# Column sums of the modulation on VectorE beside the feed-forward, and the two scan directions of the linear attention in pairs

## The chip, the cores and the metric

The kernel runs on one core of one Trainium2 chip. The metric is the time on the device of one execution, in microseconds (us), less is better.

## What is computed

Two layers of a diffusion backbone work on 256 latent tokens (x) and 256 context tokens (ctx) of width 1024. Each layer needs six modulation rows of 1024 numbers (shift, scale and gate ahead of the mixer, and the same three ahead of the feed-forward), made from a conditioning vector. Layer 0 needs them for two conditionings (c for x, c_ctx for ctx). Layer 1 drops the context after the mixer, so its last three rows are needed for c alone.

```python
def modulation(cond, w, b):
    return jnp.split(jax.nn.silu(cond) @ w + b, 6, axis=-1)
...
    for i in range(DEPTH):
        last = i == DEPTH - 1
        sh1, sc1, gt1, sh2, sc2, gt2 = [m[:, None, :] for m in modulation(c, w_ada[i], b_ada[i])]
        csh1, csc1, cgt1, csh2, csc2, cgt2 = modulation(c_ctx, w_ada[i], b_ada[i])
        h = rmsnorm(x, g_pre_mix[i]) * (1.0 + sc1) + sh1
        hc = rmsnorm(ctx, g_pre_mix[i]) * (1.0 + csc1) + csh1
        y, yc = mixer(h, hc, w_in[i], w_out[i], gla_w_gate[i], gla_b_gate[i], gla_g_norm[i], na_rpb[i], not last)
        x = x + gt1 * rmsnorm(y, g_post_mix[i])
        h = rmsnorm(x, g_pre_ffn[i]) * (1.0 + sc2) + sh2
        x = x + gt2 * rmsnorm(channel_mixer(i, h), g_post_ffn[i])
```

The mixer projects the tokens and runs two groups of heads on them: gated linear attention in chunks of 64 tokens, forward and backward in the sequence, each direction with a running state S that is scaled by a decay and added to once per chunk; and neighbourhood attention (a softmax over a window of the grid and all context keys). The channel mixer is a dense SwiGLU in layer 0 and eight SwiGLU experts, two chosen per token, in layer 1. All weights are float32.

## The kernel before

All of it is one program of five engines, each of which takes its instructions strictly in order: TensorE (PE), VectorE (DVE), ScalarE (ACT), GpSimd (POOL) and SyncE (SP), which issues nearly all transfers. A scheduler sets the order of each engine from the order in which the code is written, except in stretches that are marked as written out by hand. Two generators are interleaved by `weave(main, filler, each)`: after each `yield` of the main one, `each` steps of the filler are taken.

**Weights.** A weight arrives as a float32 piece `raw` of 128 x 1024 numbers (0.5 MB) in a ring of five buffers. For most products it is split into a rounded part `wr` (ACT, line 169) and the rest `wl` (DVE, line 170), three buffers of each, and a product of 512 columns is three matmuls (`mm3`, lines 210 to 212) with the activations' parts `HR` and `HL`.

**Modulation.** `ada_rows` (line 344) makes 512 columns of the 6144, named by j from 0 to 11: it loads four raw pieces of `w_ada` and multiplies them, unsplit, with the conditionings in `condS` on PE: eight matmuls of 32 output rows each (line 354), in float32, which the profile records twice each. `ada_cols` copies the rows (line 359), turns them into columns with four transpositions (line 371), and adds up four partial rows and the bias on DVE (lines 373, 374). `ada_gate` makes the gate (j = 4, 5 or 10, 11): the row is spread over all partitions by matmuls with `selbc` (line 418), the bias and the gain are put in on DVE and POOL (lines 420, 421). Before the change layer 1's columns are made in three places: j = 0 to 3 beside the dense feed-forward of layer 0; j = 4, 5 in layer 1's projections and linear attention; j = 6 to 9 and then 10, 11 beside layer 1's neighbourhood attention.

**Stages in order of time**, with the us of the profiled span: start (0 to 60), layer 0's projections and linear attention (60 to 200), neighbourhood attention (200 to 300), output projection (300 to 350), dense feed-forward, its first part (350 to 615) and its second (615 to 745); layer 1's projections (745 to 815), linear attention (815 to 895), neighbourhood attention (895 to 957), output projection with the router (957 to 996), experts (996 to 1898).

**Start.** `start` is written by hand: x arrives in four tiles; each is normalised (line 1881 on ACT and what follows it) and turned on PE (line 1889). The first modulation columns come in four quarters (lines 1852, 1860), each turned into scale and shift, and then the first projection begins (line 210). `clear_rel` fills a tile `far` with -1e30 and writes it over two tables in DRAM, 1.5 MB each, by GpSimd's own transfers (line 331).

**Linear attention** (`core`, in `gla_parts`). Its items are pairs of a direction d and a token tile of 128 tokens, two chunks in each. Step s1 makes decays E, s2 the products inside a chunk, s3 (line 787) adds to the output bank: values (line 797), then per chunk two matmuls with the state (line 804) and four DVE operations that advance it (line 816).

**Neighbourhood attention** (`natt`). Of an item (two heads b, one of them j, 128 queries), `n1` makes the scores (lines 899, 900), adds the window's bias (904), takes the maximum (907) and the exponential on ACT (910); `n1b` divides by the sum (916, 917); `n2` transposes (927) and copies (928); `n3` multiplies with the values (942), and `na_done` writes the result (1002, 1003). Every second pair of heads needs operands that `prep` makes (875 to 879). Layer 1 has 16 items. Its filler is `sr` (the projection r), then LAG steps of `fill`, `o_turns` (line 1056, the linear attention's output transposed), and the rest of `fill`; `RATE` says how many filler steps come after each step (their values stand in the diff below).

**Dense feed-forward**, first part: 40 pieces of weights with 24 matmuls each, two yields a piece, one filler step after each yield. **Experts**: weights stream through a ring of up to 27 buffers; the first are asked for when the output projection's last piece is at hand.

## Time and profile before

| | |
|---|---|
| median of 3 runs | 1898.14 us (1897.8 to 1899.89) |
| the profiled execution, its own time | 1900.5 us |
| its span, first to last instruction | 1898.6 us |
| PE busy | 1821.3 us, 96% of the span |
| DVE busy | 1124.8 us, 59% |
| ACT busy | 926.7 us, 49% |
| mean granted clock of TensorE | 0.989 of full speed |
| bytes moved | 492 MB, of which 352 MB are expert weights |

A matmul's recorded time contains its way through the array, so recorded times of neighbours overlap and a busy PE is a sum without the overlap. The share of an engine is an average over stages with different limits; what a stage is bound by is read from the stage.

### The profile page before, as it was taken

The numbers are of one execution on the slowest core, as the hardware profiler recorded it, in microseconds if no ns is written. First come the engines' busy times: TensorE is split into PE (matmuls) and PEld (weight loads), VectorE is DVE, ScalarE is ACT, GpSimd is POOL, SyncE is SP. The second block draws the span as 40 slices with busy tenths as digits, with TensorE's granted clock in tenths as the row PEclk, the third lists the DMA queues.
The fourth block names the chain that finished last, engine by engine and source line by source line (L and its number), as shares of the span: only waits on it lengthen the run. The fifth ranks groups of instructions, "written<-read, shape, count | busy, mean of one in ns | idle before, by whom it ended". The sixth has DMA issues, their size and how long they took to land. (4 is left out here: it accounts for less than half of the span.)

```text
span 1898.6 us, 25634 instructions
## 1 busy us (share of the span) xinstructions
PE 1821.3 (96%) x8929; PEld 1300.5 (68%) x8929; DVE 1124.8 (59%) x1636; ACT 926.7 (49%) x1336; POOL 84.6 (4%) x101
## 2 busy tenths in 40 slices
PE   5999999999999999999989999999999999999995
PEld 2687666867887887787467863488887348888731
DVE  4456876422223335367768961399997239999701
ACT  3442366522222336433647851377775237777501
POOL 2100200010000002001010000000000000000000
PEclk9999999999999999999989999999999999999998
DMA  9432645266332331434789989999999999999996
GB/s 324 136 103 52 195 166 200 78 200 199 89 100 89 114 116 53 146 90 123 243 309 358 340 319 411 413 413 409 414 381 344 411 408 413 410 413 381 342 410 254
DMA packets 203305, 492.16 MB, mean 259 GB/s; under 512 B 29665, under 2 KB 71169, under 8 KB 203169
## 3 DMA queue, kind: packets, MB, share of 16 engines
q1 hardware_dynamic: 201152, 483.12, 69.7%
q0 software_dynamic: 2016, 7.34, 1.2%
q8 instruction: 72, 1.18, 0.3%
q14 instruction: 65, 0.52, 0.1%
HBM read 486.20 MB, written 4.98 MB: 259 GB/s over the span
## 5 line engine op out<-in xcount | busy, mean ns | idle before, releaser
L170 DVE TENSOR_TENSOR wl<-raw,wr 128x1024 fp32r<-128x1024 f32 x446 | 536.6, 1227 | 227.3 <-ACT wr L169 221.6
L169 ACT ACTIVATE wr<-raw 128x1024 fp32r<-128x1024 f32 x446 | 466.3, 1059 | 301.9 <-PE ps L211 145.1
L210 PE MATMUL ps<-wr,HR 128*128 128x512 f32 x736 | 298.1, 405 | 2.7 <-ACT wr L169 2.6
L211 PE MATMUL ps<-wl,HR 128*128 128x512 f32 x736 | 291.0, 395 | 4.5 <-DVE wl L170 3.4
L212 PE MATMUL ps<-wr,HL 128*128 128x512 f32 x736 | 290.6, 395 | 0.0
L210 PE MATMUL ps<-HR,wr 128*128 128x512 f32 (+1 forms) x592 | 222.6, 377 | 9.4 <-ACT HR L1903 6.0
L211 PE MATMUL ps<-HL,wr 128*128 128x512 f32 (+1 forms) x592 | 219.6, 371 | 2.9 <-DVE HL L1908 1.5
L212 PE MATMUL ps<-HR,wl 128*128 128x512 f32 (+1 forms) x592 | 218.3, 369 | 0.0
L211 PEld LDWEIGHTS ps<-wl,HR 128*128 128x128 f32 x736 | 139.1, 189 | 41.8 <-DVE wl L170 11.4
L210 PEld LDWEIGHTS ps<-wr,HR 128*128 128x128 f32 x736 | 139.2, 189 | 37.7 <-ACT wr L169 4.9
L212 PEld LDWEIGHTS ps<-wr,HL 128*128 128x128 f32 x736 | 139.0, 189 | 32.0 <-issue 0.8
L210 PEld LDWEIGHTS ps<-HR,wr 128*128 128x128 f32 x592 | 112.1, 190 | 46.6 <-issue 15.8
L211 PEld LDWEIGHTS ps<-HL,wr 128*128 128x128 f32 x592 | 112.2, 189 | 24.1 <-DVE HL L1908 3.4
L212 PEld LDWEIGHTS ps<-HR,wl 128*128 128x128 f32 x592 | 112.2, 190 | 19.8
L1524 PE MATMUL ps<-raw,xw 128*64 128x512 f32 (+1 forms) x596 | 117.2, 537 | 1.6 <-DMA raw<-in_moe_w_gate 0.8
L210 PE MATMUL ps<-wr,tr 128*128 128x512 f32 x280 | 111.9, 400 | 0.0
L211 PE MATMUL ps<-wl,tr 128*128 128x512 f32 x280 | 110.8, 396 | 0.0
L212 PE MATMUL ps<-wr,tl 128*128 128x512 f32 x280 | 110.6, 395 | 0.0
L1539 DVE TENSOR_TENSOR hid<-hid,ps 128x512 f32<-128x512 f32 (+1 forms) x47 | 31.3, 665 | 133.0 <-PE ps L1524 133.0
L1524 PEld LDWEIGHTS ps<-raw,xw 128*64 128x64 f32 x596 | 40.7, 137 | 65.9 <-issue 53.6
L1524 PE MATMUL ps<-raw,tw 128*64 128x512 f32 x272 | 66.4, 604 | 5.7 <-DMA raw<-in_moe_w_down 4.2
L212 PEld LDWEIGHTS ps<-wr,tl 128*128 128x128 f32 x280 | 52.6, 188 | 12.8
(353 smaller groups left out, 2423.8 us busy)
## 6 DMA issues: line engine op xcount, KB each, us to landing
raw<-in_moe_w_down SPq DMA_DIRECT2D x180, 512.0 KB
raw<-in_moe_w_gate SPq DMA_DIRECT2D x169, 512.0 KB
raw<-in_moe_w_up SPq DMA_DIRECT2D x167, 512.0 KB
raw<-in_w_ada SPq DMA_DIRECT2D x80, 512.0 KB
raw<-in_w_in SPq DMA_DIRECT2D x48, 512.0 KB
HR1w<-in_moe_w_up SPq DMA_DIRECT2D x24, 512.0 KB
raw<-in_ffn_w_gate SPq DMA_DIRECT2D x22, 512.0 KB
raw<-in_ffn_w_up SPq DMA_DIRECT2D x22, 512.0 KB
```

Source lines behind the costliest of these rows:

```text
L169: nc.scalar.activation(wr, raw, AF.Copy)
L170: nc.vector.tensor_tensor(out=wl, in0=raw, in1=wr.bitcast(F32), op=ALU.subtract)
L210: nc.tensor.matmul(o, lr, rr, start=start, stop=False)
L211: nc.tensor.matmul(o, lr, rl, start=False, stop=False)
L212: nc.tensor.matmul(o, ll, rr, start=False, stop=stop)
L1524: nc.tensor.matmul(o[a * HALF:(a + 1) * HALF, 0:n], x, raw[:, a * n:(a + 1) * n], start=start, stop=stop)
L1539: nc.vector.tensor_tensor(out=hid, in0=hid, in1=st.pop((fb, 1))[:, 0:w], op=ALU.mult)
```

## The change

Four things change. **First**, layer 1's modulation columns j = 0 to 3 and 6 to 11 (not 4 and 5) leave PE: `ada_wide` takes the raw pieces beside the dense feed-forward of layer 0, and DVE multiplies each piece's 512 columns by the conditioning's number of that partition and adds it to a sum tile (lines 403, 405; one operation for each k of 8 and each conditioning: 112 in all). Four sums at a time are then added over the 128 partitions by matmuls with a tile of ones (line 409). Shifts and scales are turned as before, but for four sums at once (`wide_cols`); the gate goes through two rows in DRAM, from where it is spread over the partitions in layer 1 (`wide_gate`, `load_gate`). The 24 pieces of `w_ada` for j = 6 to 11 thereby move from layer 1's neighbourhood attention into the feed-forward; the number of pieces stays the same. **Second**, `s3` takes both directions of a step together: eight value matmuls, then for each half step the state matmuls of one direction and the other in turn. The decays are copied out of E (12 small copies on DVE), and the core has 20 yields where it had 24. **Third**, layer 1's neighbourhood attention has `RATE` (.65, 40, .65) and LAG 0, and its filler no longer has modulation in it. **Fourth**, `clear_rel` is called in the pool of the start and not ahead of it.

```diff
+    def ada_wide(pool, groups):
+        for l, js, conds, done in groups:
+            combos = [(j, c) for j in js for c in conds]
+            tiles = [pool.tile([P, D], F32, tag="t4", name="sums") for _ in range((len(combos) + 1) // 2)]
+            acc = {jc: tiles[i // 2][:, i % 2 * 512:(i % 2 + 1) * 512] for i, jc in enumerate(combos)}
+            for j in js:
+                for u in range(4):
+                    raw = wraw(kview(A["w_ada"][l], u, slice(j * 512, (j + 1) * 512)), 2)
+                    yield
+                    for kk in (2 * u, 2 * u + 1):
+                        for c in conds:
+                            i_, s_, o = raw[:, kk % 2 * 512:(kk % 2 + 1) * 512], condS[:, kk, c:c + 1], acc[j, c]
+                            if kk == 0:
+                                nc.vector.tensor_scalar(out=o, in0=i_, scalar1=s_, scalar2=None, op0=ALU.mult)
+                            else:
+                                nc.vector.scalar_tensor_tensor(out=o, in0=i_, scalar=s_, in1=o, op0=ALU.mult, op1=ALU.add)
+            yield
+            bank = ps()
+            for i, jc in enumerate(combos):
+                nc.tensor.matmul(bank[32 * i:32 * i + 32, :], ones, acc[jc], start=True, stop=True)
+            yield from done(l, js, conds, bank)
+    def wide_cols(l, js, conds, bank):
+        rows = ad.pool.tile([P, 512], F32, tag="adarows", bufs=2, name="adarows")
+        nc.scalar.activation(rows, bank, AF.Copy)
+        yield
+        pc = ps()
+        for c4 in range(4):
+            nc.tensor.transpose(pc[:, c4 * P:(c4 + 1) * P], rows[:, c4 * P:(c4 + 1) * P], ident)
+        n = len(js)
+        o = modc[l][:, 4 * js[0]:4 * js[0] + 4 * n, :].rearrange("p (j a) b -> p j a b", j=n)
+        i_ = pc.rearrange("p (a j x) -> p j a x", a=4, j=n)[:, :, :, 0:33:32] if len(conds) == 2 else \
+            pc.rearrange("p (a j x) -> p j a x", a=4, j=n)[:, :, :, 0:1].to_broadcast([P, n, 4, 2])
+        b_ = bcol[:, l, 4 * js[0]:4 * js[0] + 4 * n].rearrange("p (j a) -> p j a", j=n)
+        for q in range(n):
+            nc.vector.tensor_tensor(out=o[:, q], in0=i_[:, q], in1=b_[:, q].unsqueeze(2).to_broadcast([P, 4, 2]), op=ALU.add)
+        yield
+    gate_rows = dp.tile([2, 512], F32, name="gate_rows")
+    def wide_gate(l, js, conds, bank):
+        bb, gb = (ad.pool.tile([P, 512], F32, tag=t, bufs=n, name=t) for t, n in (("bb", 2), ("gb", 1)))
+        for i, j in enumerate(js):
+            r = slice(32 * i, 32 * i + 32)
+            nc.gpsimd.dma_start(bb[r], A["b_ada"][l:l + 1, j * 512:(j + 1) * 512].to_broadcast([32, 512]))
+            nc.gpsimd.dma_start(gb[r], A["g_post"][2 + l:3 + l, i * 512:(i + 1) * 512].to_broadcast([32, 512]))
+        yield
+        rows = ad.pool.tile([P, 512], F32, tag="adarows", bufs=2, name="adarows")
+        for t, i_ in ((bb, bank), (gb, rows)):
+            nc.vector.tensor_tensor(out=rows[0:64], in0=i_[0:64], in1=t[0:64], op=ALU.add if t is bb else ALU.mult)
+        for i in range(2):
+            nc.gpsimd.dma_start(gate_rows[i:i + 1, :], rows[32 * i:32 * i + 1, :])
+        yield
+    def load_gate(gt):
+        gt[0] = gtb()
+        nc.gpsimd.dma_start(gt[0], gate_rows.rearrange("a b -> (a b)").unsqueeze(0).to_broadcast([P, D]))
         yield
...
+                Es = gc.tile([P, 2, 2], F32, tag="Es", bufs=3, name="Es")
+                at = P + (63 if d == 0 else 0)
+                nc.vector.tensor_copy(Es, E[:, :, at:at + 65:64])
+                it["dec"] = lambda hpi, c: Es[:, hpi, c:c + 1]
...
-            def s3(it):
-                d, tt, step = it["d"], it["tt"], it["step"]
+            def values(it):
+                d, tt = it["d"], it["tt"]
...
+            def s3(pair):
+                for it in pair:
+                    values(it)
+                for i in range(2):
+                    cs = [(it, i if it["d"] == 0 else 1 - i) for it in pair]
                     for hpi in range(2):
+                        for it, c in cs:
+                            S = state[it["d"]]
+                            if it["out"] and S is not None:
+                                nc.tensor.matmul(obank[it["tt"]][64 * c:64 * c + 64, hpi * 256:(hpi + 1) * 256],
+                                                 it["qb"][:, hpi, 64 * c:64 * c + 64], S[:, hpi].rearrange("p a t -> p (a t)"),
+                                                 start=False, stop=False, skip_group_check=True)
+                    for it, c in cs:
+                        if it["step"] < 3 or i == 0:
+                            advance(it, c)
+                for it in pair:
+                    if it["out"] and seen[it["tt"]] == 2 and it["tt"] in obank:
+                        normalise(it["tt"], obank.pop(it["tt"]))
...
-                if 0 <= i - 2 < n:
-                    s3(items[i - 2])
+                if 0 <= i - 2 < n and i % 2:
+                    s3(items[i - 3:i - 1])
...
         with banks_of(0), sbuf(name="mx", bufs=1) as mx:
-            if full:
-                clear_rel(mx)
...
                     with sbuf(name="st", bufs=1) as sp:
+                        clear_rel(sp)
...
-    RATE, FILL = ((1.2, 17, .5), (1.2, 11, 1)), (5, 6)
-    LAG = 0, 6
+    RATE, FILL = ((1.2, 17, .5), (.65, 40, .65)), (5, 6)
+    LAG = 0, 0
...
-        fill = chain(ada_gate(0, 1, [0, 1], gts[0][1]), ada_cols(1, [0, 1, 2, 3]), scale_of(1, 0))
+        fill = chain(ada_gate(0, 1, [0, 1], gts[0][1]),
+                     ada_wide(t4, [(1, [0, 1], [0, 1], wide_cols), (1, [2, 3], [0, 1], wide_cols), (1, [6, 7, 8, 9], [0], wide_cols),
+                                   (1, [10, 11], [0], wide_gate)]), scale_of(1, 0))
...
-    mixer(1, fill_core, lambda early: chain(ada_cols(1, [6, 7, 8, 9]), scale_of(1, 1), early, ada_gate(1, 1, [0], gts[1][1])),
+    mixer(1, fill_core, lambda early: chain(scale_of(1, 1), load_gate(gts[1][1]), early),
```

On **POOL at the program's beginning** the fills of the linear attention's tiles (line 620, 683 after the change; klz, qez, aT and S are its tiles) stand behind the transfers of far before:

```order
L329 MEMSET far 128x384
L620 MEMSET klz_116 128x512
L331 DMA rel_93<-far 128x8x384
L331 DMA rel_94<-far 128x8x384
L620 MEMSET klz_117 128x512
```

and after the change:

```order
L683 MEMSET S_0_131 128x512
L683 MEMSET S_1_132 128x512
L331 MEMSET far 128x384
L333 DMA rel_95<-far 128x8x384
L333 DMA rel_96<-far 128x8x384
```

All ten fills now stand ahead of the two transfers, where one stood ahead of them.

On **DVE in the dense feed-forward** (line 170 makes wl for one piece of weights, line 1125, after the change 1201, multiplies the two branches of the SwiGLU; hid is their product) the rows read before:

```order
L170 TENSOR_TENSOR wl<-raw,wr 128x1024
L1125 TENSOR_TENSOR hid_3476<-hid_3476,ps 128x512
L170 TENSOR_TENSOR wl<-raw,wr 128x1024
L1125 TENSOR_TENSOR hid_3477<-hid_3477,ps 128x512
L373 TENSOR_REDUCE modc_85<-ps 128x8
```

and after it:

```order
L170 TENSOR_TENSOR wl<-raw,wr 128x1024
L405 SCALAR_TENSOR_TENSOR sums<-raw,condS,sums 128x512 x7
L170 TENSOR_TENSOR wl<-raw,wr 128x1024
L1201 TENSOR_TENSOR hid_3495<-hid_3495,ps 128x512
L403 TENSOR_SCALAR sums<-raw,condS 128x512 x2
L405 SCALAR_TENSOR_TENSOR sums<-raw,condS,sums 128x512 x2
```

Between two pieces' splits there are now up to seven operations of the sums; so it goes on for some ten pieces (64 operations, two conditionings), and then with three or four between two splits for some thirteen (48 operations, one conditioning).

On **PE in layer 1's neighbourhood attention** (K, Q and ql are the scores' operands, p the probabilities) the rows read before:

```order
L371 MATMUL ps<-cst_base,adarows 128x128 x4
L927 MATMUL ps<-cst_base,p 128x128 x4
L354 MATMUL ps<-raw,condS 32x512 x4
L899 MATMUL ps<-K_7292,Q_7294 128x512
L900 MATMUL ps<-K_7292,ql_7147 128x512
L354 MATMUL ps<-raw,condS 32x512
```

and in the same part of the stage after the change:

```order
L1004 MATMUL ps<-cst_base,p 128x128 x4
L976 MATMUL ps<-K_7450,Q_7452 128x512
L977 MATMUL ps<-K_7450,ql_7327 128x512
L1004 MATMUL ps<-cst_base,p 128x128 x4
L1019 MATMUL ps<-PT,nv_6029 64x256 x8
```

The modulation's matmuls and transpositions have left the stage; scores, transpositions and values follow each other directly.

## Rows read from the trace of the kernel before

**Rows 1.** The page, parts 1 and 2: busy us by engine, DMA by slice.

```profile
PE 1821.3 (96%) x8929; PEld 1300.5 (68%) x8929; DVE 1124.8 (59%) x1636; ACT 926.7 (49%) x1336; POOL 84.6 (4%) x101
DMA  9432645266332331434789989999999999999996
```

**Rows 2.** Windows: length, busy PE, PEld, DVE, ACT, POOL, granted clock, DMA share, GB/s.

```profile
0.00:60.00 60.00, 36.06 (x175) 20.54 (x176) 26.65 (x53) 22.25 (x42) 16.38 (x24) 0.94 0.87 287
115.00:200.00 85.00, 85.00 (x496) 67.35 (x496) 55.56 (x119) 29.12 (x58) 7.00 (x9) 1.00 0.24 61
895.00:957.00 62.00, 57.21 (x319) 29.21 (x318) 45.21 (x111) 38.73 (x80) 2.40 (x5) 1.00 0.70 236
1300.00:1500.00 200.00, 200.00 (x894) 145.28 (x894) 157.72 (x166) 131.27 (x149) 0.00 (x0) 1.00 1.00 389
```

**Rows 3.** Timelines of the start (start us, us, engine, line), and one window.

```profile
1.81 2.02 POOL L331 DMA_DIRECT2D rel<-far  x2
6.15 1.94 POOL L620 MEMSET S<- 128x512 f32 x4
...
6.45 12.19 SPq L1852 DMA_DIRECT2D raw<-in_w_ada  x8
...
15.68 1.06 ACT L1881 ACTIVATE HL<-x 128x1024 fp32r<-128x1024 f32 x1 [9.54 <-DMA x<-in_x]
...
25.55 1.06 PE L1860 MATMUL ps<-raw,condS 128*32 128x512 f32 x8
...
31.87 0.80 PE L210 MATMUL ps<-HR,wr 128*128 128x512 f32 x1 [3.85 <-ACT HR L1903]
...
12.00:16.00 4.00, 0.00 (x0) 0.00 (x0) 0.00 (x0) 0.32 (x1) 0.00 (x0) 1.00 1.02 388
```

**Rows 4.** One line's windows (us, busy PE, PEld, clock): 354; 371; 418; 354 again.

```profile
895.00:957.00 62.00, 19.82 (x96) 2.89 (x96) 1.00 0.70 236
895.00:957.00 62.00, 2.40 (x16) 1.96 (x16) 1.00 0.70 236
895.00:957.00 62.00, 1.94 (x4) 0.75 (x4) 1.00 0.70 236
400.00:460.00 60.00, 8.53 (x64) 1.26 (x64) 1.00 0.68 222
```

**Rows 5.** Groups of instructions on DVE, shapes apart: busy us, mean ns.

```profile
L1662 DVE SCALAR_TENSOR_TENSOR x<-ps,T,x 128x512 f32<-128x512 f32 x28 | 19.1, 744 | 3.0 <-PE ps L1658 3.0
L917 DVE TENSOR_SCALAR p<-p,ri 128x512 f32<-128x512 f32 x32 | 15.4, 481 | 0.1
L603 DVE SCALAR_TENSOR_TENSOR x<-u,rs_y,x 128x1024 f32<-128x1024 f32 x8 | 10.3, 1282 | 0.2
```

**Rows 6.** Dense feed-forward: one window, and DVE's longest wait from 345 to 615.

```profile
480.00:495.00 15.00, 15.00 (x66) 12.12 (x65) 4.37 (x4) 4.12 (x5) 0.00 (x0) 1.00 0.26 73
...
DVE wl L170 <- ACT wr L169: 144.0, 40, 8.1
```

**Rows 7.** Windows in layer 1's neighbourhood attention, columns as in group 2.

```profile
900.50:944.50 44.00, 41.76 (x250) 21.69 (x249) 37.46 (x96) 29.81 (x65) 0.00 (x0) 1.00 0.71 234
944.50:956.90 12.40, 10.07 (x48) 3.45 (x47) 2.50 (x4) 3.88 (x7) 2.40 (x5) 1.00 0.96 336
900.00:920.00 20.00, 17.75 (x96) 9.78 (x95) 19.04 (x47) 13.20 (x31) 0.00 (x0) 1.00 0.55 176
```

**Rows 8.** PE's timeline around the end of the same stage.

```profile
928.77 0.60 PE L927 MATMUL ps<-cst_base,p 128*128 128x128 f32 x4
929.30 1.95 PE L942 MATMUL ps<-PT,nv 128*64 128x256 f32 x16
...
956.90 0.63 PE L559 MATMUL psh<-wr,HR 128*128 128x512 f32 x2
```

**Rows 9.** PE's timeline in layer 0's linear attention.

```profile
177.59 1.09 PE L804 MATMUL ps<-S,qb 128*64 128x256 f32 x8
178.61 0.51 PE L210 MATMUL ps<-HR,wr 128*128 128x512 f32 x1
```

**Rows 10.** Windows with a less busy PE, columns as in group 2.

```profile
904.00:908.00 4.00, 2.24 (x12) 1.35 (x11) 3.87 (x10) 2.24 (x5) 0.00 (x0) 1.00 0.00 0
988.00:996.00 8.00, 5.58 (x37) 4.70 (x29) 5.14 (x18) 2.37 (x5) 0.19 (x1) 0.50 0.96 341
```

More of the change, by code (lines that the diff above doesn't have):

```diff
@@ L311 @@
     nc.gpsimd.memset(condS, 0.0)
+    ones = pers.tile([P, 32], F32, name="ones")
+    nc.gpsimd.memset(ones, 1.0)
     silu = pers.tile([P, KD, 2], F32, name="silu")
@@ new lines, in advance @@
+            def advance(it, c):
+                d = it["d"]
+                S, Sn = state[d], zget(f"S{d}")
+                for hpi in range(2):
+                    for h in range(2):
+                        r = slice(64 * h, 64 * h + 64)
+                        if S is None:
+                            nc.vector.tensor_copy(Sn[r, hpi, h, :], it["pdv"][r, hpi, c, :])
+                        else:
+                            nc.vector.scalar_tensor_tensor(
+                                out=Sn[r, hpi, h, :], in0=S[r, hpi, h, :], scalar=it["dec"](hpi, c)[r],
+                                in1=it["pdv"][r, hpi, c, :], op0=ALU.mult, op1=ALU.add)
+                state[d] = Sn
@@ L826, in normalise @@
                 nc.scalar.activation(o4, ob, AF.Square)
-                ss = gc.tile([P, 4], F32, tag="g_ss", bufs=2, name="g_ss")
+                ss = gc.tile([P, 4], F32, tag="g_ss", bufs=1, name="g_ss")
                 nc.vector.tensor_reduce(out=ss, in_=o4, axis=AX.X, op=ALU.add)
```

26 lines of the change are left out of this document (2 added, 24 removed).

## Prediction, made before the changed kernel was run

> **What bounds the kernel now.** I read the page first: PE is busy for 96% of the span, DVE for 59%, and the transfers run close to full in the last half [rows 1]. A share of 96% over the whole program says that work taken from PE should be worth its length, if nothing else becomes the limit in the stage it is taken from, so I then read the stages by windows [rows 2]. Layer 0's linear attention shows PE busy without a gap, at full clock, with transfers at 0.24: work on PE is the limit there. The start is another matter: PE is busy for 36 of 60 us and the transfers for 0.87 of the time, so the start waits for data and for chains of small operations. In layer 1's neighbourhood attention PE is busy for 57.2 of 62 us, but DVE has 45.2 us of its own: that is the next floor if PE is relieved. In the experts both PE (1.00) and the transfers (1.00) are full [rows 2]; the change doesn't touch them, and what happens ahead of them moves them as a whole.
>
> **The start.** ACT waits 9.5 us for a tile of x and gets it at 15.7 [rows 3]. What is in its way: GpSimd issues the two transfers of far, 3.15 MB, from 1.8 on, ahead of the other tiles of x. In the changed order nine more fills stand ahead of them, each 0.485 us (1.94 for four), so they are issued 4.4 us later, at about 6.2, when x's transfers are nearly all issued. At the 388 GB/s seen meanwhile [rows 3] 3.15 MB are 8.1 us: this is the most that x can gain. But the first quarter of modulation columns (2.1 MB, issued from 6.45 on) now shares the engines with far. x done at about 7.6, then 5.25 MB at 388 GB/s end at 21.1, and the quarter's last products on PE, which began at 25.55 and ended at 26.6, end near 22. First product of the projection: 31.9 before, then some 27.5. I take **4 us** of gain; the bounds are 0 (the quarter's data come no earlier) and 8.
>
> **The dense feed-forward.** Removed from PE: four j's of modulation, 8.53 us for 64 recorded matmuls [rows 4], and 16 transpositions at 2.40/16 = 0.15 us, 2.4 us. Added: 14 matmuls with ones. The trace has none of them, but line 354 has their shape (32 rows, 512 columns, four side by side); eight of those make 8.53/4 = 2.13 us, so four 1.07 and four groups 4.3; and 12 transpositions, 1.8. Net: 4.8 us less on PE.
>
> DVE gets 98 multiply-adds and 14 multiplications. The nearest row for the first is a multiply-add of 512 with one operand in PSUM, 744 ns; over 1024 numbers in SBUF it is 1282, of which half is 641; for the second, 481 [rows 5]. I take 744. Now the pace. Without modulation PE records 66 matmuls in 15 us, so a piece of 24 takes 5.45 us, and DVE is busy 4.37 of 15 us, 1.59 us a piece [rows 6]. In the ten pieces beside the first two groups DVE has 15.9 + 56 x 0.744 + 8 x 0.48 = 61.4 us; PE has 54.5 for the pieces, 2.1 for the second j of layer 0's gate, 3.2 for two groups of ones with transpositions: 59.8. DVE falls behind by 1.6 us. Its cover is the three buffers of split weights: it has waited up to 8.1 us for ACT, which waits for PE to give a buffer back [rows 6], so it runs at least one piece, 5.45 us, ahead. That hides the 112 operations; behind the sums of the second group PE's matmuls with ones wait for DVE a little sooner than for the split, and I leave 1 us for it. In the thirteen pieces of the last groups DVE has 20.7 + 48 x 0.74 = 56 us against 71 of PE. Cost without this cover: what DVE needs beyond PE is paid in full. Net of the stage: **3.8 us** gained, bounds -4 and +6. The 24 pieces of w_ada that arrive here rather than later find transfers at 0.26 [rows 6].
>
> **The linear attention.** Four state matmuls of one item now take 1.02 us from their start to the next matmul [rows 9], though two after each other write the same half of the output's partitions. In the pairs two neighbours always write different halves. The gain lies between nothing and a half: 44 such matmuls at 0.255 us are 11 us in both layers, at best 5.6 saved. Against it: all eight state matmuls of a pair now stand together on PE, and the second four need the first advance of both directions, eight DVE operations, ahead of them. DVE also makes 12 copies more; it is busy for 55.6 of 85 us there [rows 2], which hides them. I take **2 us** for both layers, bounds -2 and +5.
>
> **Layer 1's neighbourhood attention.** Six j's leave PE: 19.8 us, 16 transpositions 2.4, the gate's spreading 1.9 [rows 4], 24.1 of 57.2 us. PE's floor falls to 33 us, so DVE decides. From the first item's bias to the last item's division is the window 900.5 to 944.5: DVE is busy for 37.46 of 44 us [rows 7]. The modulation's own small operations there are about 1.4 of these (four pairs of 0.35), which leaves 36.1. In 900 to 920, where PE did not hold it up, DVE was busy for 19.04 of 20 [rows 7]; at that density 36.1 take 37.9, and the last division ends at 938.4, 6.1 us earlier. After it comes a tail. Before, it is 12.4 us long, and DVE is busy for 2.5 of them and PE with modulation for most [rows 7]: the gate of j = 10, 11 stands in front of the last values and of the output projection. What must remain is four transpositions (0.60), their copy on ACT (about as long), and the values' products, 1.95 [rows 8], with hand-overs some 3.5 us. So the output projection begins at about 942 and not at 956.9 [rows 8]: **14.9 us** gained. Bounds: 8, if only the tail goes and the items keep PE's old pace with the projection r now spread between them, and 18, if DVE's waits vanish (36.1) and the tail is 2.5. The output projection needs 8 pieces of w_out, which no longer stand behind w_ada in the ring.
>
> **The sum**: 4 + 3.8 + 2 + 14.9 = 24.7 us. The profiled execution took 1900.5 us on its own, so the profile after should show about 1876; the median of the runs is 2.4 us lower than that execution, and from 1898.1 the sum gives **1874 us**. I count all of it through the experts: they ask for their first weights when the output projection begins to end, so the stream and PE move together.
>
> **Rivals.**
> (1) **The clock falls in the relieved stage.** In 988 to 996 PE is busy for 5.58 of 8 us with small matmuls, and the granted clock is 0.50, that is 1.2 GHz; in 904 to 908 it is busy for only 2.24 of 4 and keeps 1.00 [rows 10]. Both patterns are like the relieved stage: an item takes 37.9/16 = 2.4 us of it, and leaves PE two scores' matmuls at the pitch of 5.45/24 us, 0.60 of transpositions and a quarter of 1.95, together 1.5 us. If the clock falls there, the item takes PE 3.1 us: 0.7 lost on each of the last 8 items, where the projection r no longer fills PE, are 5.6 us, and some 4 more go until the output projection has woken the clock. It ends near 1884. The Trainium skill, page "TensorE: Matmul & The Clock Gate", section "HAM oscillation — how this bites in real kernels", says that a PE which idles again and again between groups of matmuls is put back to half rate each time and pays for the wake-up each time; by that rule this rival would be the likeliest, and the time 1884. The trace agrees for 988 to 996 and not for 904 to 908.
> (2) **DVE sets the pace of the dense stage.** It does if a multiply-add costs more than (59.8 + 5.45 - 15.9 - 3.8)/56 = 0.81 us. At 1.0 us the ten pieces lose 10 us, and the time is 1884. The rows of 744 and 641 speak against it, the new in-place form on its own result for it.
> (3) **The experts swallow it.** The transfers are full there, and if the stream of weights began no earlier than now, its end would not move: about 1897. Against it: the first request is tied to the output projection, which is earlier.
> (4) **Slower.** The same place as (2) with a multiply-add that gains nothing from being half as long, 1282 ns [rows 5]: the ten pieces cost 26 us more than PE and its cover, the thirteen behind them 20.7 + 42 x 1.282 + 6 x 0.48 - 71 = 6.5, together 33 against 25.7 gained: 1905. It turns from gain to loss at about 1.2 us.
>
> **How the numbers follow.** Likeliest 0.66 at 1874, own range 1864 to 1882 from the bounds of its terms. (1) 0.13 at 1884; (2) 0.11 at 1884; (3) 0.05 at 1897; (4) 0.05 at 1905. A range of 1864 to 1888 leaves out (3), (4), and the outer parts of the rest. A change of 0.2%, 3.8 us, is about what a measurement tells from none: faster 0.90, same 0.05, slower 0.05.
>
> **What the profile after would show.** Start: x's second tile normalised at 8 to 12 rather than 15.7, the first projection's product at 26 to 29. Dense: PE without gaps, DVE busy for some 0.8 to 0.9 of each window early in the stage, and the multiply-add near 0.7 us; a wait of PE for wl or for the sums above 2 us would be rival (2). Neighbourhood attention of layer 1: DVE above 0.9, PE at 0.7 or so, clock 1.00, and 47 us from start to output projection; a clock of 0.5 in it is rival (1). Experts: as long as before, from the first expert's product to the end. Wrong would make me above all a slower sum on DVE, or a stage of items that is held by hand-overs between engines and not by DVE's work.

## The result, and the profile after

The changed kernel took **1879.79 us** (median of 6 runs, 1878.82 to 1885.11), the kernel before, measured beside it, 1897.97: a ratio of 0.990, 95% interval 0.9889 to 0.9912. That is 18.2 us where 24 were forecast. The profiled execution took 1879.96 us; its span, 1878.1, is 20.5 shorter than that of before.

Part 1 of the page of the changed kernel, beside [rows 1]: TensorE keeps its share, VectorE goes from 59 to 63%.

```profile
span 1878.1 us, 25461 instructions
PE 1797.8 (96%) x8773; PEld 1297.5 (69%) x8773; DVE 1189.9 (63%) x1750; ACT 922.7 (49%) x1329; POOL 84.2 (4%) x103
```

Where the 20.5 us came from is read from PE's timelines, from the starts of the same instructions in both traces (us of the span; the forecast is that of the sum's terms, half of the linear attention's 2 us for each layer):

| up to | before | after | gained in the stretch | forecast |
|---|---|---|---|---|
| first product of the projection | 31.9 | 31.7 | 0.2 | 4 |
| last product of layer 0's output projection | 347.9 | 347.9 | -0.2 | 1 |
| first product of the dense stage's second part | 615.3 | 606.4 | 8.9 | 3.8 |
| its last product | 739.7 | 730.4 | 0.5 | 0 |
| first bias of layer 1's neighbourhood attention (DVE) | 900.5 | 889.8 | 1.3 | 1 |
| first product of the output projection | 956.9 | 934.4 | 11.8 | 14.9 |
| last group of products of the routing | 995.1 | 971.2 | 1.4 | 0 |
| end of the span | 1898.6 | 1878.1 | -3.4 | 0 |

The total is close and the parts are not. PE's timeline of the changed kernel (start us, us, engine, line, and in brackets how long PE had stood and what ended it) has most of it:

```profile
20.64 1.92 PE L1936 MATMUL ps<-raw,condS 128*32 128x512 f32 x4 [4.06 <-DMA raw<-in_w_ada]
...
24.39 2.08 PE L1936 MATMUL ps<-raw,condS 128*32 128x512 f32 x8
...
31.66 0.80 PE L210 MATMUL ps<-HR,wr 128*128 128x512 f32 x1 [3.85 <-ACT HR L1979]
...
171.62 1.95 PE L876 MATMUL ps<-S,qb 128*64 128x256 f32 x16
173.50 0.50 PE L210 MATMUL ps<-HR,wr 128*128 128x512 f32 x1
...
226.31 0.50 PE L211 MATMUL ps<-wl,HR 128*128 128x512 f32 x1 [3.62 <-DVE wl L170]
...
426.45 1.06 PE L409 MATMUL ps<-sums,ones 128*32 128x512 f32 x8
427.45 0.50 PE L210 MATMUL ps<-HR,wr 128*128 128x512 f32 x1
...
929.95 0.70 PE L1004 MATMUL ps<-cst_base,p 128*128 128x128 f32 x4 [1.35 <-DVE p L994]
930.58 3.89 PE L1019 MATMUL ps<-PT,nv 128*64 128x256 f32 x16
934.40 0.73 PE L622 MATMUL psh<-wr,HR 128*128 128x512 f32 x2
```

At the start, x comes early (its second tile is normalised at 8.22 and not at 15.68, [rows 3]), but PE then waits 4.06 us for the first quarter of w_ada, whose last eight matmuls begin at 24.39 where they began at 25.55. They take 2.08 us where they took 1.06 [rows 3]: behind that wait the granted clock is 0.50 in 20 to 24, that is 1.2 GHz, and 0.77 in 24 to 28 (1.00 in both before). So they end only 0.1 us earlier, and the products that need them hardly move. Sixteen recorded state matmuls of a pair take 1.88 us to the next matmul; two groups of eight took 2 x 1.02 [rows 9]. At 222.7 PE stands 3.62 us for wl, a wait that before did not have. Four matmuls with ones take 1.00 us (1.07 forecast). The last products with the values in layer 1 (930.58) take 3.89 us where sixteen recorded ones took 1.95 [rows 8].

Windows of the changed kernel, columns as in [rows 2]:

```profile
12.00:16.00 4.00, 3.62 (x15) 1.58 (x14) 3.14 (x7) 2.04 (x6) 0.00 (x0) 1.00 1.05 416
20.00:24.00 4.00, 3.36 (x11) 1.73 (x12) 0.36 (x1) 0.00 (x0) 0.00 (x0) 0.50 1.05 386
400.00:420.00 20.00, 20.00 (x87) 16.23 (x86) 20.00 (x28) 6.36 (x8) 4.51 (x5) 1.00 0.75 230
420.00:440.00 20.00, 20.00 (x93) 15.43 (x93) 20.00 (x33) 4.89 (x7) 0.00 (x0) 1.00 0.78 245
460.00:480.00 20.00, 20.00 (x91) 16.44 (x90) 14.22 (x22) 4.03 (x5) 0.00 (x0) 1.00 0.85 278
889.80:929.80 40.00, 30.97 (x168) 21.56 (x166) 37.80 (x90) 29.21 (x62) 0.00 (x0) 0.87 0.19 54
929.80:934.40 4.60, 4.45 (x21) 2.79 (x21) 0.00 (x1) 0.60 (x1) 0.19 (x1) 0.63 0.64 199
```

In the dense stage VectorE is full for 40 us and PE has no gap: the cover of split weights holds. In before PE stood once in this part, for 0.87 us at its end:

```profile
615.33 0.70 PE L559 MATMUL psw<-wr,hidr 128*128 128x512 f32 x2 [0.87 <-ACT wr L169]
```

From the first bias to the last division of layer 1's neighbourhood attention VectorE is busy for 37.80 of 40 us, and the clock is at 0.87, so that rival (1) is there by its sign, and in the tail behind it (929.80 to 934.40) the clock is at 0.63. One line of VectorE in the dense stage, and the only wait of PE from 350 to 608:

```profile
L405 DVE SCALAR_TENSOR_TENSOR sums<-raw,condS,sums x98: 732/742/1777, 392.5 to 529.9; 128x512 f32<-128x512 f32 x98
```

```profile
PE ps L212 <- DVE wl L170: 0.5, 1, 0.5
```

### The profile page after: what moved, and what is told of

It is laid out like the page before. It is cut to its first block, busy times and chain, and to the rows that moved or that the text cites. A ratio compares the mean times of both kernels' runs of the same rounds, so it can differ in the third digit from the quotient of the medians.

```text
span 1878.1 us, 25461 instructions
## 1 busy us (share of the span) xinstructions
PE 1797.8 (96%) x8773; PEld 1297.5 (69%) x8773; DVE 1189.9 (63%) x1750; ACT 922.7 (49%) x1329; POOL 84.2 (4%) x103
## 5 line engine op out<-in xcount | busy, mean ns | idle before, releaser
L405 DVE SCALAR_TENSOR_TENSOR sums<-raw,condS,sums 128x512 f32<-128x512 f32 x98 | 71.6, 761 | 19.6 <-DMA raw<-in_w_ada 18.8
```

The costliest lines, as they stand in the source:

```text
L405: nc.vector.scalar_tensor_tensor(out=o, in0=i_, scalar=s_, in1=o, op0=ALU.mult, op1=ALU.add)
```

## The experiments

Four theories had to be told apart: why the start gave nothing (bytes, or a chain of small operations), what the pairs do, whether VectorE or the clock sets layer 1's neighbourhood attention, and why the dense stage gave twice the forecast and the experts took some back. Unless said otherwise an experiment is the changed kernel with one edit, times are medians, and shifts are starts of the same instruction against the first profile of the changed kernel. Ratios are to the kernel before as measured beside that experiment, with 95% intervals. How far one profile can be trusted: eight of the profiles here are of kernels with the same layer 0, and their first product of the projection lies between 30.4 and 32.8, their last scores of layer 0 between 294.3 and 296.4, of which the first profile is the earliest.

**The changed kernel again** (no edit).

> The changed kernel once more, nothing edited, as the base for the runs beside it and for one question: in its profile a matmul of 512 columns followed the one before it after 0.2289 us in 450 to 600, in the profile of before after 0.2333, both at a granted clock of 1.00. Theory 1, the pitch belongs to the execution and not to the change: this profile shows other values between 0.228 and 0.234 in the same stretches, and the part of the dense stage's gain that goes with it (960 matmuls x 0.0044 us = 4.2 us) comes and goes. Theory 2, the pitch belongs to the kernel (VectorE or the transfers beside it): 0.2289 again in 450 to 600 and 0.233 in the experts. Time 1878 to 1882 in either case.

1879.4 us, ratio 0.9895 (0.9879 to 0.9912). The pitch of 512-column matmuls, from the starts in stretches of 30 us, is 0.2289 to 0.2294 again in 450 to 600 and 0.2324 to 0.2330 in most of the experts, and all points of the table up to the routing lie within 0.5 us of the first profile (the end 1.2 later): theory 2, the pitch belongs to the program. Two rows each, nine matmuls apart, of before (2.10 us) and of the changed kernel (2.06), both at clock 1.00:

```profile
559.69 0.39 PE L210 MATMUL ps<-HR,wr 128*128 128x512 f32 x1
...
561.79 0.40 PE L210 MATMUL ps<-HR,wr 128*128 128x512 f32 x1
```

```profile
559.74 0.39 PE L210 MATMUL ps<-HR,wr 128*128 128x512 f32 x1
...
561.80 0.39 PE L210 MATMUL ps<-HR,wr 128*128 128x512 f32 x1
```

**far issued late.**

```diff
-                        clear_rel(sp)
                         start(sp, [G["v4"], nv4], *proj_T(w, 0, 4, [NT] * 4, G["qk_after"]))
...
+                    if full:
+                        clear_rel(ge)
                     G["gates_load"](ge)
```

> The two transfers of far are issued after the start instead of 6.4 us into it. Theory 1, the start is held by bytes: the shares of the transfers are over 1.0 from 12 to 40 us, so 3.15 MB less ahead of the first quarter's last pieces are worth up to 8 us at the 388 to 416 GB/s seen there; the first projection product begins at 24 to 28 instead of 31.7, layer 0's second rope at 105 to 108 instead of 112, time 1873 to 1876. Rival A, later quarters of w_ada and the weights give it back or far collides with layer 0's projections: product early, rope at 111 to 112, time 1879 to 1880. Rival B, the chain of small operations behind x holds the start: the first product stays at 31 or so, time 1880.

1876.0 us, ratio 0.9877 (0.986 to 0.9893). far's transfers are issued at 46.7 and 56.4. PE's timeline:

```profile
17.33 1.05 PE L1937 MATMUL ps<-raw,condS 128*32 128x512 f32 x4
...
19.34 1.06 PE L1937 MATMUL ps<-raw,condS 128*32 128x512 f32 x8
21.15 0.66 PE L1947 MATMUL ps<-cst_base,adarows 128*128 128x128 f32 x4 [0.75 <-ACT adarows L1942]
25.66 0.80 PE L210 MATMUL ps<-HR,wr 128*128 128x512 f32 x1 [3.85 <-ACT HR L1980]
```

The first product comes 6.0 us earlier, so bytes hold the start (theory 1, rival B falls). Some 3.3 us of it are the second piece of the quarter, which PE takes at 17.33 and not at 20.64; the other 2.8 are the clock: from there to the quarter's last product PE needs 3.1 us, at 1.00, where the changed kernel needed 5.8, at 0.50 in 20 to 24 and 0.77 in 24 to 28. But 3.8 are left at layer 0's first state matmul and 2.0 at its last scores: rival A in part.

**The directions one after the other.** The core has 24 filler steps again, and `s3(it)` does for its item `values`, then for each of its two chunks the state matmuls and `advance`.

```diff
-                if 0 <= i - 2 < n and i % 2:
-                    s3(items[i - 3:i - 1])
+                if 0 <= i - 2 < n:
+                    s3(items[i - 2])
                     yield
```

> The linear attention's two directions are taken one after the other again, as before the change; the rest is the changed kernel. In the pairs eight recorded pairs of state matmuls took 1.88 us from the first to the next matmul where two single ones took 2 x 1.02. Theory 1, pairs are worth next to nothing on TensorE (0.16 us for each of five or six pairs, some 0.9 us): 1880 to 1882, layer 0's last product of the output projection at most 0.6 us later. Theory 2, the pairs let layer 1's neighbourhood attention begin earlier (its first bias came 10.7 us earlier where the last rope came 7.7 us earlier): 1882 to 1884, the loss in layer 1 alone. Theory 3, the pairs cost, since eight state matmuls wait for both advances: 1876 to 1879.

1875.9 us, ratio 0.9877 (0.9861 to 0.9894): theory 3, the pairs cost 3.5 us (runs of 1874.3 to 1877.7 against 1878.7 to 1881.3). Layer 0's last scores come 2.6 us earlier; of that 1.7 are left at the end of the dense stage. Layer 1's output projection comes 4.5 us earlier: from the first bias to it are 41.4 us and not 44.6, in a stage that this edit does not touch. PE's longest wait around 222 is 1.1 us. What made it 3.6 is on VectorE and GpSimd of the changed kernel (one row of GpSimd, two of VectorE):

```profile
217.16 0.58 POOL L473 DMA_DIRECT2D bb<-in_b_ada  x1
```

```profile
223.84 1.29 DVE L483 TENSOR_TENSOR gtb<-ps,bb 128x512 f32<-128x512 f32 x2 [3.89 <-DMA bb<-in_b_ada]
225.04 3.45 DVE L170 TENSOR_TENSOR wl<-raw,wr 128x1024 fp32r<-128x1024 f32 x2
```

With 20 filler steps instead of 24, the last ones of the filler (layer 0's gate) come bunched behind the core. The second half's bias is asked for at 217.16, VectorE stands in order before its addition, the split weights queue behind it, and PE behind these.

**The pairs with 24 filler steps.**

```diff
                     s3(items[i - 3:i - 1])
                     yield
+                    yield
```

> The pairs stay, but after each of the four pairs two filler steps are taken instead of one, so that the core has 24 again. With the directions apart the kernel was 3.5 us faster; in the changed kernel PE waits 3.6 us for wl at 222 us, VectorE stands at the gate's bias add and waits 3.9 us for bb. Theory 1, the bunched filler is what the pairs cost: PE's wait at 222 falls to under 1 us, the last scores of layer 0 come 2 to 3 us earlier, time 1875 to 1877. Theory 2, the order of the state matmuls itself costs: 1879 to 1880, with the waits as they are.

1877.3 us, ratio 0.9882 (0.9867 to 0.9896). The wait for bb is gone (VectorE's addition stands at 216.99 with no wait) and the last scores come 1.8 us earlier. But PE waits for wr in the same place now, so that the bunching moved and didn't vanish:

```profile
220.59 0.80 PE L210 MATMUL ps<-wr,HR 128*128 128x512 f32 x1 [2.91 <-ACT wr L169]
```

Theory 1 in part: its signs are there, each somewhat short of what it asked for. Of the 1.8 us 0.6 are left at the end of the dense stage; what the kernel gains at its end comes from layer 1's neighbourhood attention, where the output projection begins 3.8 us earlier. PE's timeline and two windows there:

```profile
927.97 2.70 PE L1020 MATMUL ps<-PT,nv 128*64 128x256 f32 x16
930.60 0.73 PE L622 MATMUL psh<-wr,HR 128*128 128x512 f32 x2
```

```profile
889.33:927.27 37.94, 28.90 (x166) 20.53 (x164) 36.46 (x87) 27.08 (x61) 0.19 (x1) 0.91 0.26 81
927.27:930.60 3.33, 3.07 (x20) 1.66 (x21) 0.33 (x1) 1.17 (x3) 0.00 (x0) 1.00 0.00 0
```

VectorE's timeline of the changed kernel shows what is different there:

```profile
926.28 1.21 DVE L170 TENSOR_TENSOR wl<-raw,wr 128x1024 fp32r<-128x1024 f32 x1
...
928.20 1.20 DVE L170 TENSOR_TENSOR wl<-raw,wr 128x1024 fp32r<-128x1024 f32 x1
929.33 0.48 DVE L994 TENSOR_SCALAR p<-p,ri 128x512 f32<-128x512 f32 x1
```

In both kernels three splits of w_out stand among the items, one of them at 918.99 and 918.44. In the changed kernel the other two stand in front of the last two divisions; PE stands for 0.67 and 1.35 us there, the clock falls, and the last products take 3.8 us to the output projection. In this run no split stands in the last 8 us of the items, and these products take 2.6 us at clock 1.00. From the first bias to the output projection are 41.3 us for 44.6; 1.0 of the difference are three operations for keys and queries that stand ahead of the first bias here. The directions apart (41.4) and the experiment after this one (41.1) have the same order; another profile of the changed kernel (44.7), far late (44.8) and one matmul with ones more (44.7) have the changed kernel's. Why VectorE's order differs no run shows. So the pairs' 3.5 us are the fewer filler steps as far as this run goes (2.1 by the medians, 2.5 by the ratios), mostly by way of layer 1; whether the rest is the order of the state matmuls stays open, since the intervals overlap.

**The gate of j = 4, 5 the same way.** The fifth group has rows of its own in DRAM, and its gain comes from the row of g_post for j = 4, 5.

```diff
-                                   (1, [10, 11], [0], wide_gate)]), scale_of(1, 0))
+                                   (1, [10, 11], [0], wide_gate), (1, [4, 5], [0], wide_gate)]), scale_of(1, 0))
...
-        fill_core = ada_gate(1, 0, [0], gts[1][0])
+        fill_core = load_gate(gts[1][0], 0)
```

> The gate of j = 4, 5 of layer 1 goes the way of the others too: eight more pieces of w_ada are multiplied and summed on VectorE beside the dense feed-forward, behind the last group (545 to 600, where VectorE was busy for 5 to 6.4 of 20 us), and the row is spread from DRAM in layer 1. PE loses 4.05 us of sums and 1.78 of spreading in 740 to 900 and gains two matmuls with ones, 0.6 us. Theory 1, PE bounds layer 1's projections and linear attention: 5 us less, time 1874 to 1876, the second part of the dense stage unchanged. Rival, the linear attention of layer 1 is held by its chain over VectorE, ScalarE and PE and these products stood in gaps: 1878 to 1880. VectorE in 540 to 600 goes from 5 to 6 of 20 us to 9 or 10, PE waits for nothing new.

1878.5 us, ratio 0.9886 (0.9869 to 0.9902), not to be told from the changed kernel. From the dense stage's end to the output projection 8.7 us are gained: the 5.2 of PE's work up to the first bias, and 3.6 from VectorE's other order behind it. But the first dense part is 4.7 us longer. VectorE waits for pieces of w_ada there (29.7 us in sum for line 405, 18.8 in the changed kernel), the split weights stand behind it, and PE waits at 512.75, for 0.80 us at 555, and for 0.87 at the end of the part:

```profile
512.75 0.50 PE L212 MATMUL ps<-HR,wl 128*128 128x512 f32 x1 [1.98 <-DVE wl L170]
```

The stage has VectorE to spare on average and is still not free.

**Columns j = 6 to 11 back on TensorE in layer 1**, with the old `RATE` and `LAG`.

```diff
-    mixer(1, fill_core, lambda early: chain(scale_of(1, 1), load_gate(gts[1][1]), early),
+    mixer(1, fill_core, lambda early: chain(ada_cols(1, [6, 7, 8, 9]), scale_of(1, 1), early, ada_gate(1, 1, [0], gts[1][1])),
```

> Layer 1's columns j = 6 to 11 are back on TensorE beside layer 1's neighbourhood attention, with the old rates and lag; j = 0 to 3 stay on VectorE, and so do the pairs and far. From the first scores to the first product of the output projection were 68.4 us before and 52.0 in the changed kernel. Theory 1, these products on PE made the difference: 64 to 68 us again, the first part of the dense stage 3 us shorter than in the changed kernel (two groups with ones and transpositions less), time 1889 to 1893. Theory 2, the new rates and the order of the core did part of it: 57 to 62 us, time 1882 to 1886.

1890.9 us, ratio 0.9952 (0.9937 to 0.9966). From the first scores to the output projection 65.4 us against 52.1, and the first dense part, from the end of the output projection, is 3.7 shorter: theory 1. Moving these six j's together with the rates made for it is worth 11 us, most of the change; what the rates do by themselves no run shows.

**Keys and queries on GpSimd**, for pairs 1 to 3 of heads in layer 1.

```diff
+                side = nc.vector if full or b < 1 else nc.gpsimd
-                nc.vector.tensor_tensor(out=K2[j][other], in0=nk[own, b, :], in1=K2[j][own].bitcast(F32), op=ALU.subtract)
+                side.tensor_tensor(out=K2[j][other], in0=nk[own, b, :], in1=K2[j][own].bitcast(F32), op=ALU.subtract)
```

and so for the two operations behind it.

> The three operations that make the keys and queries of pairs 1 to 3 of heads in layer 1's neighbourhood attention (K 0.685 us, Q 0.29, ql 0.42) go to GpSimd: 6.4 us less on VectorE from 890 to 930. Theory 1, VectorE sets the pace (busy 9.7 to 9.97 of 10 us in 890 to 900 and 910 to 930): the last division comes 4 to 6 us earlier, time 1874 to 1876. Theory 2, the clock of PE (0.66 and 0.83 in two of these windows) sets it: the stage stays at 40 us from the first bias to the last division, time 1879 to 1880. Rival, GpSimd is late with them (2.33 us for 128 x 1024 numbers, so an estimated 1.2 for K) and the next pair waits: 1880 to 1884.

1876.9 us, ratio 0.9867 (0.9852 to 0.9883). First bias 890.3, last division done at 927.4, 37.1 us against 40.0, and 40.4 against 44.6 to the output projection, at clock 1.00 throughout. The last division comes 2.4 us earlier where theory 1 asked for 4 to 6. VectorE sets the pace, but of the 6.4 us taken from it in this stretch 2.9 came back, and not all of that is GpSimd's: this run also has VectorE's other order (last products 2.6 us, tail 3.3), with which three runs took 37.7 to 38.1 and 41.1 to 41.4 us without GpSimd. Against those it gives about 0.8. Ahead of the first bias, where five more of these operations stood, the run is 3.7 us shorter, more than their 2.0; why that is no run shows. Why moving them gives so little behind the bias, its timeline and GpSimd's at 897 show:

```profile
897.25 0.41 DVE L982 TENSOR_TENSOR ps<-ps,B 128x256 f32<-128x256 f32 x1
897.57 1.32 DVE L995 TENSOR_SCALAR p<-p,ri 128x512 f32<-128x512 f32 x1
...
902.53 1.99 DVE L170 TENSOR_TENSOR wl<-raw,wr 128x1024 fp32r<-128x1024 f32 x1
```

```profile
897.32 1.29 POOL L955 TENSOR_TENSOR K<-nk,K 64x512 fp32r<-64x512 f32 x1
```

A division of 0.48 us takes 1.32 and a split of 1.21 takes 1.99 while GpSimd works; operations with an operand in PSUM (0.41, 0.68) keep their time. The Trainium skill, page "GPSIMD Engine Reference", section "1. Specifications", says that GpSimd shares its way to SBUF with VectorE and contends with instructions that read two SBUF inputs or run in a two-port mode. The trace agrees for the split, which has two inputs in SBUF; in which mode the division runs no row shows.

**A busier TensorE in the same stage.**

```diff
+            for _ in range(0 if full else 2):
+                nc.tensor.matmul(pS[:, :n], Q2[j][:, tok], K2[j][:, NT - n:NT], start=True, stop=True)
             nc.tensor.matmul(pS[:, :n], Q2[j][:, tok], K2[j][:, NT - n:NT], start=True, stop=False)
```

> In layer 1's neighbourhood attention the first matmul of each item's scores is made three times instead of once: 32 more matmuls of 0.233 us, 7.5 us of PE, which has about 10 us idle or at half clock in 880 to 930. Theory 1, the fall of the clock costs time there (0.66 and 0.83 in two windows of 10 us): PE stays at 1.00 and the stage from the first scores to the output projection goes from 52.0 to 48 to 50 us, time 1876 to 1878. Theory 2, VectorE sets the pace and the clock is only a sign of PE's idle: the clock rises or not, the stage stays at 51.5 to 53 us, time 1879 to 1881. Rival, the added work stands in PE's way: 54 to 58 us, 1882 to 1886.

```profile
888.60:928.60 40.00, 34.85 (x204) 25.50 (x203) 37.77 (x90) 30.21 (x65) 0.00 (x0) 0.99 0.20 60
927.60:933.10 5.50, 4.51 (x20) 2.74 (x20) 0.42 (x1) 1.46 (x3) 0.19 (x1) 0.69 0.47 154
```

The clock is 0.99 instead of 0.87, VectorE is busy for 37.77 us (37.80 in the changed kernel), and from the first bias (888.7) to the output projection (933.1) it takes 44.4 us against 44.6: theory 2 for the items, where VectorE sets the pace. They take 38.8 us for 40.0, so that the low clock cost at most 1.2 there. It does not settle the tail: there the clock is at 0.69, the last products take 3.8 us as in the changed kernel, PE waits 0.93 us for HL, and the tail is 5.6 us for 4.6. What a full clock is worth in the tail is seen in the pairs with 24 filler steps: 1.2 us (2.6 for 3.8). The median, 1883.7 (ratio 0.9911, 0.9896 to 0.9926; runs from 1879.2 to 1885.3), does not speak for a gain either; it lies in the rival's band, but the profile ends only 0.8 us behind that of the changed kernel and does not show where more would be lost.

**Half as many sums again on VectorE.**

```diff
+                            if kk % 2:
+                                nc.vector.scalar_tensor_tensor(out=o, in0=i_, scalar=condS[:, kk, 31:32], in1=o, op0=ALU.mult, op1=ALU.add)
```

> Beside every second multiply-add of the sums stands one more that adds zero times the piece to the same sum: 56 more on VectorE, 0.742 us each, 41.6 us; the sums and all else stay. By the step of the prediction on the dense stage: in the ten pieces beside the first two groups VectorE has 15.9 + 88 x 0.742 + 8 x 0.48 = 85.0 us where PE has 59.8 and the buffers of split weights hide 5.45, so 19.8 us are lost; in the thirteen behind them 20.7 + 66 x 0.742 + 6 x 0.48 = 72.6 against 71, 1.6 more. Theory 1, that step holds: the dense stage 18 to 24 us longer, PE waits for wl by about as much, time 1898 to 1904. Theory 2, the ring of raw pieces and the idle of VectorE behind the sums hide more: under 12 us, time under 1892.

1895.3 us, ratio 0.9975 (0.9965 to 0.9985). From the output projection's end the dense part is 15.8 us longer where the step gives 21.4, and PE waits now:

```profile
420.00:440.00 20.00, 18.30 (x74) 11.97 (x73) 18.65 (x29) 4.84 (x5) 0.00 (x0) 1.00 0.58 183
460.00:480.00 20.00, 13.94 (x44) 7.17 (x42) 18.51 (x26) 4.37 (x5) 0.00 (x0) 0.84 0.56 176
```

```profile
PE ps L212 <- DVE wl L170: 5.2, 2, 3.8
PE ps L411 <- DVE sums L407: 2.6, 2, 1.7
```

Neither theory's range holds the result (18 to 24 us and 1898 to 1904; under 12 and 1892), but the step's kind of wait is there. Read by the step, the cover is some 5.6 us larger than the 5.45 taken for it; that reading is an estimate. By it the stage still has some 9 us of VectorE's time to spare (61.4 us of work against 59.8 of PE and 11.0 of cover), and a multiply-add could cost 0.9 us and not 0.81 before VectorE takes the stage over.

**One matmul with ones more**, in the first group.

```diff
-                nc.tensor.matmul(bank[32 * i:32 * i + 32, :], ones, acc[jc], start=True, stop=True)
+                for _ in range(2 if jc == (1, 1) and l else 1):
+                    nc.tensor.matmul(bank[32 * i:32 * i + 32, :], ones, acc[jc], start=True, stop=True)
```

> One of the first four matmuls with ones is made twice; nothing else. The pitch of the same 512-column matmuls was 0.2333 us until some 427 us, where the first of them stands, and 0.2289 after it, in each of the five profiles of changed kernels, 0.2333 there in before. Theory 1, the pitch hangs on where the matmuls lie in PE's stream: 0.233 after 427 us or another value, and the dense stage up to 4 us longer, with a shift of the pitch in the experts too, time 1876 to 1884. Theory 2, it hangs on something that this doesn't move (buffers, banks, the engines beside it): 0.2289 again, time 1879 to 1881.

1880.4 us, ratio 0.99 (0.9886 to 0.9915); the pitch is 0.2333 until 426.8 and 0.229 after it, as in the changed kernel: theory 2. A single matmul more in PE's stream does not move it.

**Three edits together**: far late, GpSimd for keys and queries, and the directions apart (first) or the pairs with 24 steps (second).

> Three edits together: far after the start, the two directions one after the other, and keys and queries of pairs 1 to 3 in layer 1 on GpSimd. Alone they were at 1876.0, 1875.9 and 1876.9 where the changed kernel was at 1879.4 to 1880.4. Theory 1, they lie in three stages and add up (3.4 + 3.5 + 2.5 to 3): 1869 to 1871. Rival, what far gives in the start is given back in layer 0's neighbourhood attention (its gain fell from 6.0 to 2.0 us along layer 0) or the full transfers of the experts take it: 1873 to 1876.

> The same with the pairs kept and a filler step more after each, in place of the directions apart. The pairs with 24 steps were at 1877.3, the directions apart at 1875.9. If state matmuls in pairs save what they showed (0.16 us for eight) and nothing else differs, the two come out within 1 us of each other: 1869 to 1872. If eight state matmuls waiting for both advances cost: 1 to 2 us slower than with the directions apart.

1868.6 us, ratio 0.9838 (0.9825 to 0.9852), and **1867.4 us**, ratio 0.9827 (0.9813 to 0.984): both beat the changed kernel, by 11 to 12 us, and can't be told from each other. Both lie just below what adding up asked for; the rival falls. The edits alone were worth 3.4, 2.1 and 2.5 with the pairs by medians, 8.0 in sum, but 3.4, 2.5 and 5.3 by the ratios to before, 11.2 in sum against 12.9 for the three: that they help each other does not follow from the totals. In layer 0 it shows in the profiles: at its last scores far alone kept 2.0 of 6.0 us and the pairs' steps alone gave 1.8, and with both the first product comes 7.4 earlier and the last scores 7.8.

## Why the prediction came out as it did

The forecast (1874, range 1864 to 1888) was near the time because errors of both signs met, which is luck: the start, the linear attention, the neighbourhood attention and the experts gave less, the dense stage more.

- **Start: the step failed.** "x done at about 7.6, then 5.25 MB at 388 GB/s end at 21.1": x was early, but the quarter was not. From 12 to 40 us the transfers are full (1.02 to 1.10), and besides far and the quarter they carry a piece of w_in and the second quarter, which the step left out of the bytes. The step also took PE's part behind the wait at full clock; PE had stood for 4.06 us, the clock was 0.50, and the 1.2 us by which the last eight matmuls began earlier went into their own length. Moving far by 4.4 us gave nothing; taking it out of the stretch gave 6.0 us. 0 was the term's lower bound.
- **Dense feed-forward: the mechanism was right, and its prices** (742 ns for 744, 1.00 us for 1.07, 0.5 us of waiting for 1). Rivals (2) and (4) fall. By the starts of all of PE's instructions, the 8.9 us measured are 3.8 by the step (4.35 of work less for 4.8, and 0.55 of waiting), 0.9 from a wait for wr at the end of the part that before had and the changed kernel has not, and 4.2 from the same 960 products, which nobody forecast: about 3.4 of these are the pitch, some 770 products behind 427 us at 0.2289 and not 0.2333. One reading was slightly off: 66 recorded matmuls in 15 us are not all of them, and at 0.2333 a piece of 24 takes 5.60 us and not 5.45, so that PE had 1.5 us more for VectorE to hide in over ten pieces.
- **Linear attention: wrong in sign.** The matmuls' saving was 0.16 us a pair, near the lower end. The Trainium skill, page "TensorE: Matmul & The Clock Gate", section "Part 3: Packing small matmuls — row/col tiling", lets matmuls with few output rows run side by side on different columns of the array; these halves of 64 rows did not (16 recorded ones of 256 columns in 1.88 us). What cost was what the change also did, four filler steps less: in layer 0 a bunched gate, a late bias on GpSimd's queue, VectorE and PE behind it. The pairs as written lose 3.5 us where 2 were to be gained. Most of that is not lost in the linear attention: with the directions apart 1.7 us were gained up to the end of the dense stage, and 3.2 from the first bias to the output projection of layer 1.
- **Layer 1's neighbourhood attention: the step was right, 3.1 us too large.** 41.5 us were forecast from the first bias to the output projection, 44.6 came, and 41.1 to 41.4 in the three runs with VectorE's other order. The items took 40.0 for 37.9: VectorE had 37.8 us of work there and not 36.1, among it one split of w_out more than before (three for two, 1.2 us) and two operations more for keys and queries (1.1). The tail took 4.6 for 3.5: two of the splits stand in front of the last divisions, PE stands there, and the last products run at clock 0.63.
- **Rival (1)** happened (0.66 in 890 to 900, with PE busy for 6.33 of 10 us; 0.83 in 910 to 920), and its price was not where it looked for it. Among the items VectorE sets the pace, and the low clock cost 1.2 us or less; the 5.6 us on the last eight items did not come. In the tail PE is on the path, and there it cost 1.2 us. For the "some 4 more" until the clock is back the prediction names no row, and the output projection behind the tail is not longer for it (24.6 us from its first product to its last, 25.0 before).
- **Experts.** "I count all of it through the experts" lost 3.4 us; 1.4 had been gained in the output projection (0.4) and the routing behind it. The pitch of 512-column products there, from the starts in 1230 to 1410, was 0.2300 to 0.2321 before and is 0.2326 to 0.2329 now. Summed over the experts, some 2440 of them take 567.8 us where they took 564.2, 3.6 more; PE's waits are not longer (13.0 us for 14.4). So the loss lies in these products, and it takes back what the pitch gave in the dense stage. Two effects of the pitch that nobody forecast thus cancel, and that was luck too.

## What to carry to other kernels

Work taken off the busiest engine is worth what the next engine leaves: count that engine's own list for the stage, with the work that now arrives earlier (a third split), and look at what stands last in it: two splits in front of the last divisions made the next engine stand, and its clock fell just where it came onto the path. Then see whether a cheap third engine slows it by sharing SBUF. When code is regrouped, count its yields as well as its operations, since a filler that is bunched can put a late transfer in front of everything queued on an in-order engine, and can shift the order of a stage far behind it. A transfer that is moved within a stretch in which the transfers are full only trades places; it must leave the stretch.

## What the runs showed of the hardware that was not expected

The same stream of 512-column matmuls runs at two paces, 0.2289 and 0.2333 us each, both at granted clock 1.00. Which of them holds is fixed for a stretch of a program (the same in all profiles of changed kernels, switching at the first matmuls with ones: near 427 us, and near 419 in the two runs of three edits, where these come earlier) and differs between programs. It is 2% of such a stage, as much as the dense term itself. One matmul more did not move it; its cause stays open.
